# Sample attention: the new positions of a batch as columns of its first block of past positions

## The chip, the cores and the metric

The kernel runs on one core of a Trainium2 chip. Its engines work side by side, each in the order of its own instructions: PE (matrix products and turns), DVE and ACT (element work), POOL (element work and indirect loads), SP (issues loads). The metric is the device time of one launch in microseconds (us), less is better.

## The reference

One inference step of a two-layer decoder, for a prompt of 1024 positions and for a sample group of 8 batches with 8 new positions each. The change touches the second layer's attention of the sample group, which has 8 heads, so 64 query rows in a batch (8 heads by 8 positions). Keys are a latent part of 256 and a rotary part of 64, from 8192 past positions (a paged cache) and the new ones:

```python
def mla_attend(q_lat, q_rope, ckv, kr):
    nq, nk = q_lat.shape[1], ckv.shape[1]
    s = jnp.einsum('bqhc,bkc->bhqk', q_lat, ckv) + jnp.einsum('bqhr,bkr->bhqk', q_rope, kr)
    visible = jnp.arange(nk)[None, :] <= (nk - nq + jnp.arange(nq))[:, None]
    s = jnp.where(visible, s.astype(jnp.float32) * SM_SCALE, -jnp.inf)
    pr = jax.nn.softmax(s, axis=-1).astype(ckv.dtype)
    return jnp.einsum('bhqk,bkc->bqhc', pr, ckv)
...
past_ckv = cache_ckv[page_table, j].reshape(bsz, n_past, KV_LORA).astype(ckv.dtype)
o_lat = mla_attend(q_lat, q_rope, jnp.concatenate([past_ckv, ckv], axis=1),
                   jnp.concatenate([past_kr, kr], axis=1))
```

## The kernel before

`sample_attention` works through items (b, J): batch b, block J. Blocks 0 to 7 are 1024 past positions each, and block 8 holds the new positions (64 columns, those of all batches, with `mnew` masking all but the batch's own); it comes first in its batch. So 72 items. A number is kept as a high and a low part (`split`, `lo`; a low part is the number less its high part), so most products are made of several matmuls. The softmax runs over the blocks with a running maximum and sum, kept as columns of `sts`.

An item is cut into pieces, each a few instructions:
- `f` (POOL) gathers a block 2 items ahead into `raws`; `na` (ACT) and `np` (POOL) copy its high part into `khi`, `lp` (POOL, L2216, two halves of 128x1024) its low part into `klo`.
- `t0`, `t1` (PE, L2226) turn the two halves of the latent keys, `tr` (L2241) the rotary keys, into PSUM; `h0`, `h1`, `hr` (ACT) copy the high parts out, `l0`, `l1`, `lr` (DVE, `lo`, L216) the low parts. lr's row reads `L216 ... fieldC<-ps,fieldC 64x1024`. The three turns take two wide PSUM buffers in turn, so t1 needs the buffer that the tr before it filled, when hr and lr have read it.
- `s0`, `s1` (PE) are the scores of 512 columns each; `c0`, `c1` (ACT) copy the half of the low parts out, `m0`, `m1` (DVE, L2286) add and take the maximum; `nm` (DVE, L2291) turns it into the exponent's bias, `ex` (ACT, L2296) is the exponent with its sum, `al`, `ac` the factor for what came before, `su` (ACT, L2308) the running sum.
- `pt` (PE, L2321) turns the probabilities into the one "pt" buffer of PSUM, `ph` (ACT, L2326) and `pl` (DVE) read them out, `pv` (PE, L2342) multiplies with the values, `o` (DVE, L2350) adds to the batch's output.
- After block 7, `e0` (DVE, L2360 to L2362) divides by the sum, `e1`, `ec`, `e2` turn the result and store it.

The order of the pieces is one table for all engines, and in each step piece x with number d works on the item d steps back. Each engine then works strictly in that order:

```python
"m1.4 l0.2 t1.2 ph.5 pv.6 nm.4 h1.2 s0.3 l1.2 na.3 tr.2 pl.5 s1.3 ex.4 o.6 e1.8 ec.8 t0.1 e2.8 "
"f.0 np.3 hr.2 e0.6 c0.3 c1.3 su.5 ac.5 lr.2 pt.4 al.4 lp.3 h0.1 m0.3"
```

So in one step e0 of a batch's last item (6 steps back) stands on DVE ahead of lr (2 steps back), and `su` of the next item (5 steps back) stands between them. `np` overwrites what pv three blocks earlier read, and waits for it. The end of the attention overlaps with the first loads and casts of the output projection (`then`; L225 and L226 are its split).

Of the kernel before, what the change touches and what calls it, by code (L numbers as in the profile page):

```python
# [20 lines left out]
P = 128  # L21
# [1633 lines left out]
class Layer1(Layer0):  # L1655
# [501 lines left out]
    def sample_attention(self, then):  # L2157
# [15 lines left out]
        L = slice(64, 128)  # L2173
        items = [(b, J) for b in range(NB) for J in (8, 0, 1, 2, 3, 4, 5, 6, 7)]
        blk = {it: n for n, it in enumerate(it for it in items if it[1] < 8)}

# [4 lines left out]

        def piece(name, new=True):


            def add(f):
                def run(n):
                    b, J = items[n]
                    if J < 8 or new:
                        f(n, b, J, blk.get(items[n]))

                pieces[name] = run
                return f

            return add


        @piece("f", False)
        def _(n, b, J, i):
            if i > 1:
                self.gather(i)  # L2200
# [3 lines left out]

        @piece("na", False)
        def _(n, b, J, i):
            nc.scalar.copy(khi[i % 3][:, :on_a], raws[i % 4][:, :on_a])  # L2207

        @piece("np", False)
# [3 lines left out]
        @piece("lp", False)  # L2213
        def _(n, b, J, i):
            for c in (slice(0, 1024), slice(1024, 2048)):
                nc.gpsimd.tensor_tensor(klo[i % 3][:, c], raws[i % 4][:, c], khi[i % 3][:, c], op=ALU.subtract)  # L2216


        for k in range(2):

            @piece(f"t{k}", False)
# [6 lines left out]
            @piece(f"h{k}", False)  # L2228
            def _(n, b, J, i, k=k):
                nc.scalar.copy(kT[i % 2][0][:, k], live[n, "t", k])  # L2230

            @piece(f"l{k}", False)
            def _(n, b, J, i, k=k):
                self.lo(kT[i % 2][1][:, k], live[n, "t", k], kT[i % 2][0][:, k])

        @piece("tr", False)
# [7 lines left out]
        @piece("hr", False)  # L2244
        def _(n, b, J, i):
            nc.scalar.copy(rT[i % 2][:64], live[n, "t", 2][:64])  # L2246

        @piece("lr", False)
        def _(n, b, J, i):
            self.lo(rT[i % 2][64:], live[n, "t", 2][:64], rT[i % 2][:64])  # L2250


        stat = lambda n, j: sts[n % 4][:, j : j + 1]
        width = lambda J: 1024 if J < 8 else NS
        for a in range(2):
            cs = slice(a * 512, a * 512 + 512)

            @piece(f"s{a}", a == 0)
            def _(n, b, J, i, a=a, cs=cs):
                W = 512 if J < 8 else NS  # L2260
                ps = live[n, "s", a] = self.ps("s")[:, :W]
                for k in range(2):
                    for t in range(2):
                        x = kT[i % 2][t][:, k, cs] if J < 8 else ckN[:, t, k]
                        nc.tensor.matmul(ps, q(k, b), x, start=k + t == 0, stop=False)  # L2265
                qr = QRs[:, b].rearrange("p s m -> p (s m)")
                if J < 8:
                    nc.tensor.matmul(ps, qr, rT[i % 2][:, cs], start=False, stop=True)  # L2268
                else:
                    for t in range(2):  # L2270
                        nc.tensor.matmul(ps, qr[:64], krN[:64, t], start=False, stop=t == 1)

            @piece(f"c{a}", a == 0)
            def _(n, b, J, i, a=a, cs=cs):
                o = sb[n % 3][H, cs][:, : min(512, width(J))]
                nc.scalar.copy(o, live[n, "s", a][L])

            @piece(f"m{a}", a == 0)
            def _(n, b, J, i, a=a, cs=cs):

                o, ps = sb[n % 3][H, cs][:, : min(512, width(J))], live[n, "s", a]
                if J == 8:
                    tt(o, o, mnew[H, b], op=ALU.add)
                first = -3e38 if J == 8 else stat(n, 5)[H] if a else stat(n - 1, 2)[H]
                out = stat(n, 2 if a or J == 8 else 5)
                V.tensor_tensor_reduce(o, ps[H], o, op0=ALU.add, op1=ALU.max, accum_out=out[H], scale=1.0, scalar=first)  # L2286

# [5 lines left out]
        @piece("ex")  # L2293
        def _(n, b, J, i):
            o = sb[n % 3][H, : width(J)]
            nc.scalar.activation(o, o, AF.Exp, bias=stat(n, 0)[H], scale=SCALE, accum_out=stat(n, 4 if J == 8 else 3)[H])  # L2296

        @piece("al", False)
        def _(n, b, J, i):
            nc.scalar.activation(stat(n, 1)[H], stat(n - 1, 0)[H], AF.Exp, bias=stat(n, 0)[H], scale=-1.0)  # L2300

        @piece("ac", False)
        def _(n, b, J, i):
            V.tensor_copy(stat(n, 1)[L], stat(n, 1)[H])

        @piece("su", False)
        def _(n, b, J, i):
            nc.scalar.activation(stat(n, 4)[H], stat(n - 1, 4)[H], AF.Identity, bias=stat(n, 3)[H], scale=stat(n, 1)[H])  # L2308


        def spans(n, J):
            nt, K = (8, P) if J < 8 else (1, NS)
            P3 = PTb[n % 3].rearrange("p (t s q) -> p t s q", t=8, s=2)
            return nt, K, P3[:K, :nt, 0], P3[:K, :nt, 1]

        @piece("pt")
        def _(n, b, J, i):
            nt, K, *_ = spans(n, J)
            ps = self.ps("pt")
            for t in range(nt):  # L2320
                nc.tensor.transpose(ps[:K, t * 64 : t * 64 + 64], sb[n % 3][H, t * P : t * P + K], self.ident[H, H])  # L2321
            live[n, "p"] = ps[:K, : nt * 64].rearrange("p (t q) -> p t q", t=nt)

        @piece("ph")
        def _(n, b, J, i):
            nc.scalar.copy(spans(n, J)[2], live[n, "p"])  # L2326

        @piece("pl")
        def _(n, b, J, i):
            *_, hi, lo = spans(n, J)  # L2330
            self.lo(lo, live[n, "p"], hi)

        @piece("pv")
        def _(n, b, J, i):
            o = live[n, "o"] = self.ps("o")[:, :256]
            PT = PTb[n % 3]
            for t in range(8 if J < 8 else 1):
                for s in range(2):
                    x, y = PT[:, t * P : t * P + P], (khi, klo)[s][(i or 0) % 3][:, t * 256 : t * 256 + 256]
                    if J == 8:  # L2340
                        x, y = PT[:NS, :P], self.kn[:NS, s]
                    nc.tensor.matmul(o, x, y, start=t + s == 0, stop=t + s == (8 if J < 8 else 1))  # L2342

        @piece("o")
        def _(n, b, J, i):
            O = oa[b % 2]
            if J == 8:
                nc.scalar.copy(O, live[n, "o"])
            else:
                V.scalar_tensor_tensor(O, O, stat(n, 1), live[n, "o"], op0=ALU.mult, op1=ALU.add)  # L2350
# [4 lines left out]

        @piece("e0", False)
        @last
# [5 lines left out]

        @piece("e1", False)
        @last
# [164 lines left out]
```

## Time and profile before

| what | value |
|---|---|
| three runs | 3080.94, 3076.39, 3082.41 us (median 3080.94) |
| the profiled execution | 3075.58 us, span of its instructions 3073.8 us |
| granted clock of PE, mean | 0.981 |
| busy over the span | PE 97%, DVE 75%, ACT 52%, POOL 41% |
| sample attention | about 1680 to 2210 us of the span |

The profiled execution is one launch, 5.4 us below the median. A busy share over the whole span mixes stages with different limits, so the attention is read by itself. PE's busy time counts matmuls that overlap as one stretch.

### The profile page before, as it was taken

The page shows a single profiled execution, that of the slowest core. Times are in us where ns is not written, and L with a number is a line of the kernel's source. Part 1 is how long each engine was busy: PE and PEld are TensorE (multiplying, and loading weights), DVE is VectorE, ACT ScalarE, POOL GpSimd, SP SyncE. Part 2 cuts the span into 40 slices and gives each one's busy share as a digit, 9 for nine tenths or more (in the row PEclk, how much of TensorE's full clock was granted, in tenths as well). Part 3 has the DMA queues.
Part 4 walks back from the last instruction along what each step waited for, and adds up shares of the span by engine and source line. Part 5 has one row for each costly group of instructions (what it writes and reads, how often), then busy time and mean ns, then how long its engine had stood idle before and what let it go on. Part 6 is the DMA issues. An engine that isn't in the chain of part 4 may idle for free.

```text
span 3073.8 us, 51474 instructions
## 1 busy us (share of the span) xinstructions
PE 2977.0 (97%) x19503; PEld 2698.0 (88%) x19503; DVE 2299.1 (75%) x4068; ACT 1608.3 (52%) x2917; POOL 1254.5 (41%) x1207
## 2 busy tenths in 40 slices
PE   8999999899999999999999999999998999999998
PEld 7888787899999887798998888888877999998887
DVE  8753656898988776647666877777758988987766
ACT  3434644544444444345555888888735444444432
POOL 1652530466665100001112988888503666662000
PEclk9999899899999999999999999999999999999999
DMA  3223132222222676511002444444532222225775
GB/s 142 73 56 113 53 131 75 77 78 71 85 78 77 203 230 230 176 52 31 30 30 95 172 161 149 156 173 169 188 103 70 85 78 71 81 74 185 230 230 187
DMA packets 147884, 364.71 MB, mean 119 GB/s; under 512 B 28028, under 2 KB 83516, under 8 KB 139444
## 3 DMA queue, kind: packets, MB, share of 16 engines
q1 hardware_dynamic: 136336, 276.40, 27.7%
q0 software_dynamic: 9216, 83.89, 7.6%
q8 instruction: 153, 2.51, 0.3%
q10 hardware_dynamic: 2084, 1.14, 0.1%
q14 instruction: 95, 0.78, 0.1%
HBM read 302.07 MB, written 58.11 MB: 117 GB/s over the span
## 4 chain that ended last, share of the span: by engine, by line
PE 82%; DVE 7%; ACT 6%; DMA 3%; POOL 1%; issue 1%; ACTq 0%; SPq 0%; DVEq 0%; POOLq 0%
PE ps L211 20%; PE ps L212 20%; PE ps L213 20%; PE ps L2342 4%; PE ps L2265 3%; PE ps L2226 3%; DMA fieldF<-w_dn 2%; PE ps L2241 2%; DVE fieldC L216 1%; ACT fieldC L2246 1%; PE ps L514 1%; PE ps L2024 1%; PE ps L1993 1%; PE ps L2321 1%; PE ps L2268 1%
## 5 line engine op out<-in xcount | busy, mean ns | idle before, releaser
L211 PE MATMUL ps<-fieldC,fieldE 128*128 128x512 f32 (+2 forms) x916 | 338.7, 370 | 4.2 <-ACT fieldC L225 2.3
L212 PE MATMUL ps<-fieldC,fieldE 128*128 128x512 f32 (+2 forms) x916 | 338.5, 370 | 2.7 <-DVE fieldC L226 2.7
L213 PE MATMUL ps<-fieldC,fieldE 128*128 128x512 f32 (+2 forms) x916 | 338.4, 370 | 1.1 <-DVE fieldE L216 1.1
L212 PE MATMUL ps<-fieldB,fieldE 128*128 128x272 f32 (+4 forms) x872 | 276.0, 317 | 0.0
L226 DVE TENSOR_TENSOR fieldC<-fieldF,fieldC 128x1024 fp32r<-128x1024 f32 x132 | 161.3, 1223 | 124.5 <-ACT fieldC L225 123.8
L225 ACT CAST fieldC<-fieldF 128x1024 fp32r<-128x1024 f32 x132 | 138.4, 1051 | 198.5 <-DMA fieldF<-w_dn 173.0
L211 PEld LDWEIGHTS ps<-fieldC,fieldE 128*128 128x128 f32 x916 | 173.0, 189 | 33.3 <-ACT fieldC L225 3.6
L212 PEld LDWEIGHTS ps<-fieldC,fieldE 128*128 128x128 f32 x916 | 172.7, 189 | 31.4 <-DVE fieldC L226 4.1
L213 PEld LDWEIGHTS ps<-fieldC,fieldE 128*128 128x128 f32 x916 | 172.8, 189 | 30.4 <-DVE fieldE L216 2.6
L211 PE MATMUL ps<-fieldA,fieldE 128*128 128x362 f32 (+4 forms) x560 | 181.1, 325 | 7.7 <-ACT fieldA L940 7.4
L213 PE MATMUL ps<-fieldA,fieldE 128*128 128x362 f32 (+4 forms) x560 | 181.7, 324 | 0.0
L216 DVE TENSOR_TENSOR fieldC<-ps,fieldC 64x1024 fp32r<-64x1024 f32 (+4 forms) x145 | 127.8, 882 | 69.4 <-ACT fieldC L2246 63.8
L212 PEld LDWEIGHTS ps<-fieldB,fieldE 128*128 128x128 f32 x872 | 169.1, 194 | 1.8 <-DVE fieldB L941 0.5
L216 DVE TENSOR_TENSOR fieldE<-fieldF,fieldE 128x512 fp32r<-128x512 f32 (+4 forms) x265 | 137.0, 533 | 41.5 <-ACT fieldE L499 28.8
L216 DVE TENSOR_TENSOR fieldD<-ps,fieldE 128x1024 fp32r<-128x1024 f32 x128 | 154.8, 1215 | 8.7 <-ACT fieldE L2230 8.7
L420 DVE SCALAR_TENSOR_TENSOR fieldD<-fieldD,fieldF 128x480 f32<-128x480 f32 (+1 forms) x176 | 145.0, 860 | 19.4 <-ACT fieldD L418 19.4
L420 DVE SCALAR_TENSOR_TENSOR fieldA<-fieldA,fieldF 128x480 f32<-128x480 f32 (+1 forms) x176 | 144.7, 858 | 19.6 <-ACT fieldA L418 19.6
L211 PE MATMUL ps<-fieldC,fieldH 128*128 128x272 f32 x528 | 153.9, 291 | 3.3 <-ACT fieldC L346 2.9
L212 PE MATMUL ps<-fieldC,fieldH 128*128 128x272 f32 x528 | 154.0, 292 | 1.8 <-DVE fieldC L347 1.8
L2216 POOL TENSOR_TENSOR fieldB<-fieldA,fieldB 128x1024 fp32r<-128x1024 f32 x64 | 152.4, 2399 | 3.8 <-ACT fieldB L2207 1.4
L213 PE MATMUL ps<-fieldC,fieldH 128*128 128x272 f32 x528 | 153.4, 291 | 0.0
L211 PE MATMUL ps<-fieldB,fieldE 128*128 128x272 f32 (+2 forms) x488 | 146.6, 301 | 0.9 <-ACT fieldA L291 0.8
(705 smaller groups left out, 10160.4 us busy)
## 6 DMA issues: line engine op xcount, KB each, us to landing
fieldF<-w_dn SPq DMA_DIRECT2D x132, 512.0 KB, 3.8
fieldF<-w_up SPq DMA_DIRECT2D x44, 512.0 KB, 3.6
fieldF<-act SPq DMA_DIRECT2D x88, 192.0 KB, 4.1
fieldA<-w_up SPq DMA_DIRECT2D x22, 512.0 KB, 3.5
fieldD<-w_up SPq DMA_DIRECT2D x22, 512.0 KB, 3.6
fieldF<-w_in SPq DMA_DIRECT2D x16, 512.0 KB, 4.3
fieldF<-w_out SPq DMA_DIRECT2D x32, 256.0 KB, 3.2
xm<-fieldC SPq DMA_DIRECT2D x16, 512.0 KB, 2.6
```

Source lines behind the costliest of these rows:

```text
L211: mm(out, wh, xh, start=first, stop=False, **kw)
L212: mm(out, wh, xl, start=False, stop=False, **kw)
L213: mm(out, wl, xh, start=False, stop=last, **kw)
L216: self.nc.vector.tensor_tensor(out, full, hi, op=ALU.subtract)
L225: self.nc.scalar.copy(hi, raw)
L226: (eng or self.nc.vector).tensor_tensor(lo, raw, hi, op=ALU.subtract)
L420: V.scalar_tensor_tensor(y[:, :n], x[:, tap : tap + n], c(tap), y[:, :n], op0=ALU.mult, op1=ALU.add)
L2216: nc.gpsimd.tensor_tensor(klo[i % 3][:, c], raws[i % 4][:, c], khi[i % 3][:, c], op=ALU.subtract)
L2226: nc.tensor.transpose(ps[:, t * P : t * P + P], raws[i % 4][:, c : c + P], self.ident)
L2241: nc.tensor.transpose(ps[:64, t * P : t * P + P], raws[i % 4][:, c : c + 64], self.ident)
L2265: nc.tensor.matmul(ps, q(k, b), x, start=k + t == 0, stop=False)
L2342: nc.tensor.matmul(o, x, y, start=t + s == 0, stop=t + s == (8 if J < 8 else 1))
```

## The change

Block 8 is no item of its own any more: 64 items. Its work goes into the pieces of block 0:
- `s0` of block 0 first makes the 64 columns of scores of the new positions in an "s" buffer, copies and masks them into `sn`, takes their maximum as column 7, from which block 0's maximum goes on.
- `ex` of block 0 makes a second exponent over `sn` (sum in column 6); `su` of block 0 adds columns 3 and 6 on DVE (L2307), where blocks 1 to 7 still use ACT; `al` and `ac` fall away for block 0.
- `pt` of block 0 turns `sn` first, copies the two parts into `PTn`, then turns the eight tiles of the block, out of the same "pt" buffer.
- `pv` of block 0 has two matmuls more; `o` of block 0 is a copy by ACT, as it was for block 8.
- `sts` has 6 buffers in place of 4.

The diff, cut to its core:

```diff
-        items = [(b, J) for b in range(NB) for J in (8, 0, 1, 2, 3, 4, 5, 6, 7)]
-        blk = {it: n for n, it in enumerate(it for it in items if it[1] < 8)}
+        items = [(b, J) for b in range(NB) for J in range(8)]
...
+        stat = lambda n, j: sts[n % 6][:, j : j + 1]
+
+        def added(o, ps, first, out):
+
+            V.tensor_tensor_reduce(o, ps[H], o, op0=ALU.add, op1=ALU.max, accum_out=out[H], scale=1.0, scalar=first)
+
         for a in range(2):
             cs = slice(a * 512, a * 512 + 512)
 
-            @piece(f"s{a}", a == 0)
+            @piece(f"s{a}")
             def _(n, b, J, i, a=a, cs=cs):
-                W = 512 if J < 8 else NS
-                ps = live[n, "s", a] = self.ps("s")[:, :W]
+                qr = QRs[:, b].rearrange("p s m -> p (s m)")
+                if a == J == 0:
+                    ps, o = self.ps("s")[:, :NS], sn[H]
+                    for k in range(2):
+                        for t in range(2):
+                            nc.tensor.matmul(ps, q(k, b), ckN[:, t, k], start=k + t == 0, stop=False)
+                    for t in range(2):
+                        nc.tensor.matmul(ps, qr[:64], krN[:64, t], start=False, stop=t == 1)
+                    nc.scalar.copy(o, ps[L])
+                    tt(o, o, mnew[H, b], op=ALU.add)
+                    added(o, ps, -3e38, stat(n, 7))
+                ps = live[n, "s", a] = self.ps("s")
                 for k in range(2):
                     for t in range(2):
-                        x = kT[i % 2][t][:, k, cs] if J < 8 else ckN[:, t, k]
-                        nc.tensor.matmul(ps, q(k, b), x, start=k + t == 0, stop=False)
-                qr = QRs[:, b].rearrange("p s m -> p (s m)")
-                if J < 8:
-                    nc.tensor.matmul(ps, qr, rT[i % 2][:, cs], start=False, stop=True)
-                else:
-                    for t in range(2):
-                        nc.tensor.matmul(ps, qr[:64], krN[:64, t], start=False, stop=t == 1)
-
-            @piece(f"c{a}", a == 0)
+                        nc.tensor.matmul(ps, q(k, b), kT[i % 2][t][:, k, cs], start=k + t == 0, stop=False)
+                nc.tensor.matmul(ps, qr, rT[i % 2][:, cs], start=False, stop=True)
+
+            @piece(f"c{a}")
             def _(n, b, J, i, a=a, cs=cs):
-                o = sb[n % 3][H, cs][:, : min(512, width(J))]
-                nc.scalar.copy(o, live[n, "s", a][L])
-
-            @piece(f"m{a}", a == 0)
+                nc.scalar.copy(sb[n % 3][H, cs], live[n, "s", a][L])
+
+            @piece(f"m{a}")
             def _(n, b, J, i, a=a, cs=cs):
-
-                o, ps = sb[n % 3][H, cs][:, : min(512, width(J))], live[n, "s", a]
-                if J == 8:
-                    tt(o, o, mnew[H, b], op=ALU.add)
-                first = -3e38 if J == 8 else stat(n, 5)[H] if a else stat(n - 1, 2)[H]
-                out = stat(n, 2 if a or J == 8 else 5)
-                V.tensor_tensor_reduce(o, ps[H], o, op0=ALU.add, op1=ALU.max, accum_out=out[H], scale=1.0, scalar=first)
+                first = stat(n, 5) if a else stat(n - 1, 2) if J else stat(n, 7)
+                added(sb[n % 3][H, cs], live[n, "s", a], first[H], stat(n, 2 if a else 5))
...
         @piece("ex")
         def _(n, b, J, i):
-            o = sb[n % 3][H, : width(J)]
-            nc.scalar.activation(o, o, AF.Exp, bias=stat(n, 0)[H], scale=SCALE, accum_out=stat(n, 4 if J == 8 else 3)[H])
-
-        @piece("al", False)
+            for o, j in ((sb[n % 3][H], 3), (sn[H], 6))[: 1 if J else 2]:
+                nc.scalar.activation(o, o, AF.Exp, bias=stat(n, 0)[H], scale=SCALE, accum_out=stat(n, j)[H])
+
+        @piece("al")
         def _(n, b, J, i):
-            nc.scalar.activation(stat(n, 1)[H], stat(n - 1, 0)[H], AF.Exp, bias=stat(n, 0)[H], scale=-1.0)
-
-        @piece("ac", False)
+            if J:
+                nc.scalar.activation(stat(n, 1)[H], stat(n - 1, 0)[H], AF.Exp, bias=stat(n, 0)[H], scale=-1.0)
+
+        @piece("ac")
         def _(n, b, J, i):
-            V.tensor_copy(stat(n, 1)[L], stat(n, 1)[H])
-
-        @piece("su", False)
+            if J:
+                V.tensor_copy(stat(n, 1)[L], stat(n, 1)[H])
+
+        @piece("su")
         def _(n, b, J, i):
+            if J == 0:
+                tt(stat(n, 4)[H], stat(n, 3)[H], stat(n, 6)[H], op=ALU.add)
+                return
             nc.scalar.activation(stat(n, 4)[H], stat(n - 1, 4)[H], AF.Identity, bias=stat(n, 3)[H], scale=stat(n, 1)[H])
...
+        def spans(PT, nt, K=P):
+            v = PT.rearrange("p (t s q) -> p t s q", t=nt, s=2)
+            return v[:K, :, 0], v[:K, :, 1]
+
+        def turned(x, nt, K=P):
+            ps = self.ps("pt")
+            for t in range(nt):
+                nc.tensor.transpose(ps[:K, t * 64 : t * 64 + 64], x[:, t * P : t * P + K], self.ident[H, H])
+            return ps[:K, : nt * 64].rearrange("p (t q) -> p t q", t=nt)
 
         @piece("pt")
         def _(n, b, J, i):
-            nt, K, *_ = spans(n, J)
-            ps = self.ps("pt")
-            for t in range(nt):
-                nc.tensor.transpose(ps[:K, t * 64 : t * 64 + 64], sb[n % 3][H, t * P : t * P + K], self.ident[H, H])
-            live[n, "p"] = ps[:K, : nt * 64].rearrange("p (t q) -> p t q", t=nt)
+            if J == 0:
+                self.split(*spans(PTn, 1, NS), turned(sn[H], 1, NS))
+            live[n, "p"] = turned(sb[n % 3][H], 8)
...
         @piece("pv")
         def _(n, b, J, i):
             o = live[n, "o"] = self.ps("o")[:, :256]
             PT = PTb[n % 3]
-            for t in range(8 if J < 8 else 1):
+            for t in range(8):
                 for s in range(2):
-                    x, y = PT[:, t * P : t * P + P], (khi, klo)[s][(i or 0) % 3][:, t * 256 : t * 256 + 256]
-                    if J == 8:
-                        x, y = PT[:NS, :P], self.kn[:NS, s]
-                    nc.tensor.matmul(o, x, y, start=t + s == 0, stop=t + s == (8 if J < 8 else 1))
+                    y = (khi, klo)[s][i % 3][:, t * 256 : t * 256 + 256]
+                    nc.tensor.matmul(o, PT[:, t * P : t * P + P], y, start=t + s == 0, stop=J > 0 and t + s == 8)
+            for s in range(0 if J else 2):
+                nc.tensor.matmul(o, PTn[:NS], self.kn[:NS, s], start=False, stop=s == 1)
 
         @piece("o")
         def _(n, b, J, i):
             O = oa[b % 2]
-            if J == 8:
+            if J == 0:
                 nc.scalar.copy(O, live[n, "o"])
             else:
                 V.scalar_tensor_tensor(O, O, stat(n, 1), live[n, "o"], op0=ALU.mult, op1=ALU.add)
...
-        sts = [g("F^", 8) for _ in range(4)]
+        sts = [g("F^", 8) for _ in range(6)]
         sb = [g("F^", 1024) for _ in range(3)][::-1]
+        sn = g("F^", NS)
         PTb = [g("C", 1024) for _ in range(3)]
+        PTn = g("C", P)
```

The rows below show each engine's order in the new program and the old one. A name like `ps_17489` is a PSUM buffer, `fieldF_67` holds the columns of `sts` and the output sums (and `sn` in the new program), `fieldC_11912` the low and turned parts, `fieldH_9936` the scores and probabilities.

DVE, in the step in which one batch ends and the next begins. Before, from the low part of the last t0 to lr:

```order
L216 TENSOR_TENSOR fieldD_4497<-ps_17396,fieldE_4493 128x1024
L216 TENSOR_TENSOR fieldC_11912<-ps_17388,fieldC_11912 64x64
L2350 SCALAR_TENSOR_TENSOR fieldF_67<-fieldF_67,ps_17406 128x256
L2360 RECIPROCAL fieldF_67<-fieldF_67 64x1
L2361 COPY fieldF_67<-fieldF_67 64x1
L2362 TENSOR_SCALAR fieldF_67<-fieldF_67 128x256
L216 TENSOR_TENSOR fieldC_11912<-ps_17433,fieldC_11912 64x1024
```

And now:

```order
L216 TENSOR_TENSOR fieldD_4497<-ps_17452,fieldE_4493 128x1024
L216 TENSOR_TENSOR fieldC_11912<-ps_17437,fieldC_11912 128x8x64
L2354 SCALAR_TENSOR_TENSOR fieldF_67<-fieldF_67,ps_17462 128x256
L2364 RECIPROCAL fieldF_67<-fieldF_67 64x1
L2365 COPY fieldF_67<-fieldF_67 64x1
L2366 TENSOR_SCALAR fieldF_67<-fieldF_67 128x256
L2307 TENSOR_TENSOR fieldF_67<-fieldF_67 64x1
L216 TENSOR_TENSOR fieldC_11912<-ps_17489,fieldC_11912 64x1024
```

Between e0's scaling and lr stands the addition of block 0's two sums, and the low part of the probabilities ahead of `o` is a whole block's instead of the 64x64 piece.

PE, in the step that turns the probabilities of a batch's new positions, and DVE's part of it. Before, on PE:

```order
L2226 MATMUL ps_17371<-ident,fieldA_15833 128x128 x8
L2321 MATMUL ps_17388<-ident,fieldH_9936 64x64
L2226 MATMUL ps_17396<-ident,fieldA_15833 128x128 x8
```

Now, on PE, and under it DVE's rows from lr on:

```order
L2220 MATMUL ps_17416<-ident,fieldA_15833 128x128 x8
L2319 MATMUL ps_17433<-ident,fieldF_67 64x64
L2319 MATMUL ps_17437<-ident,fieldH_9936 128x64 x8
L2220 MATMUL ps_17452<-ident,fieldA_15833 128x128 x8
...
L216 TENSOR_TENSOR fieldC_11912<-ps_17397,fieldC_11912 64x1024
L216 TENSOR_TENSOR fieldC_11912<-ps_17433,fieldC_11912 64x64
```

The single turn and the eight turns follow each other on PE with the same buffer, and DVE's reading of the first stands behind lr.

ACT, at the end of the attention (the last exponents, and casts of the output projection, L225). Before:

```order
L2326 CAST fieldC_11912<-ps_21603 128x8x64
L225 CAST fieldA_21700<-fieldH_9936 128x1024
L2296 ACTIVATE fieldH_9936,fieldF_67<-fieldH_9936,fieldF_67 64x1024
L2308 ACTIVATE fieldF_67<-fieldF_67 64x1
L2300 ACTIVATE fieldF_67<-fieldF_67 64x1
```

And now:

```order
L2330 CAST fieldC_11912<-ps_21563 128x8x64
L225 CAST fieldE_4493<-fieldF_67 128x512
L2292 ACTIVATE fieldH_9936,fieldF_67<-fieldH_9936,fieldF_67 64x1024
L2309 ACTIVATE fieldF_67<-fieldF_67 64x1
L2297 ACTIVATE fieldF_67<-fieldF_67 64x1
L225 CAST fieldA_21660<-fieldH_9936 128x1024
```

The cast into fieldA, which overwrites what POOL's lp reads, has gone behind the last exponent, and a cast into fieldE stands ahead of it.

## Rows read from the trace of the kernel before

**Rows 1.** Windows: start:end, length, then busy time by engine, clock, DMA

```profile
1796.98:1862.51 65.53, 63.43 (x477) 56.22 (x476) 51.97 (x98) 56.21 (x95) 55.91 (x33) 1.00 0.45 162
```

**Rows 2.** Waits of PE: for whom, us in total, times, longest us

```profile
PE ps L2226 <- DVE fieldC L216: 13.6, 16, 1.0
```

**Rows 3.** In order of time, PE and ACT, one batch: start, us, instruction [idle before]

```profile
1875.43 1.09 PE L2226 MATMUL ps<-ident,fieldA 128*128 128x128 f32 x8 [0.83 <-DVE fieldC L216]
1882.42 0.24 PE L2321 MATMUL ps<-ident,fieldH 64*64 64x64 f32 x1
1882.81 1.09 PE L2226 MATMUL ps<-ident,fieldA 128*128 128x128 f32 x8
1883.82 0.21 ACT L2326 CAST fieldC<-ps 64x64 fp32r<-64x64 f32 x1
1905.91 1.09 PE L2226 MATMUL ps<-ident,fieldA 128*128 128x128 f32 x8 [1.00 <-DVE fieldC L216]
```

**Rows 4.** In order of time, PE, POOL and DVE, one regular step

```profile
1913.57 1.09 PE L2226 MATMUL ps<-ident,fieldA 128*128 128x128 f32 x8
1914.42 2.16 PE L2342 MATMUL ps<-fieldB,fieldC 128*128 128x256 f32 x16
1916.55 1.28 POOL L2211 TENSOR_SCALAR fieldB<-fieldA 128x1280 fp32r<-128x1280 f32 x1 [1.57 <-PE ps L2342]
1917.78 0.47 DVE L2350 SCALAR_TENSOR_TENSOR fieldF<-fieldF,ps 128x256 f32<-128x256 f32 x1
1917.91 4.72 POOL L2216 TENSOR_TENSOR fieldB<-fieldA,fieldB 128x1024 fp32r<-128x1024 f32 x2
1919.69 1.22 DVE L216 TENSOR_TENSOR fieldC<-ps,fieldC 64x1024 fp32r<-64x1024 f32 x1 [1.27 <-ACT fieldC L2246]
1921.22 0.98 PE L2226 MATMUL ps<-ident,fieldA 128*128 128x128 f32 x7
```

**Rows 5.** In order of time, the scaling of e0 and POOL's low part

```profile
1885.83 4.77 POOL L2216 TENSOR_TENSOR fieldE<-fieldA,fieldD 128x1024 fp32r<-128x1024 f32 x2
1887.57 0.80 DVE L2362 TENSOR_SCALAR fieldF<-fieldF 128x256 f32<-128x256 f32 x1
...
2211.40 0.35 DVE L2362 TENSOR_SCALAR fieldF<-fieldF 128x256 f32<-128x256 f32 x1
```

**Rows 6.** In order of time, other stages; then two group lines (least/median/most ns; busy, mean ns)

```profile
110.54 1.44 POOL L914 TENSOR_TENSOR fieldG<-fieldF,T 128x512 f32<-128x512 f32 x1 [1.52 <-DVE fieldC L918]
110.98 1.02 DVE L919 TENSOR_TENSOR fieldC<-fieldG,fieldD 128x4 f32<-128x4 f32 x1
...
646.35 0.71 DVE L420 SCALAR_TENSOR_TENSOR fieldA<-fieldA,fieldF 128x480 f32<-128x480 f32 x1
646.38 1.91 POOL L434 TENSOR_TENSOR fieldA<-fieldA 128x544 f32<-128x544 f32 x1 [1.41 <-ACT fieldA L433]
646.99 1.58 DVE L430 SCALAR_TENSOR_TENSOR fieldA<-fieldA,fieldF 128x64 f32<-128x64 f32 x2
...
L919 DVE TENSOR_TENSOR fieldC<-fieldG,fieldD x4: 151/168/1017, 111.0 to 244.6; 128x4 f32<-128x4 f32 x4
...
L2304 DVE COPY fieldF<-fieldF 64x1 f32<-64x1 f32 x64 | 9.4, 147 | 1.4
```

**Rows 7.** Waits of PE in order of time, and windows of low clock behind two

```profile
241.97 1.27 PE L1171 MATMUL ps<-fieldD,fieldG 64*128 64x136 f32 x4 [2.61 <-DVE fieldG L1158]
...
241.47:251.71 10.24, 9.74 (x36) 8.49 (x37) 7.26 (x17) 1.32 (x3) 5.41 (x6) 0.50 0.42 102
2200.72:2207.54 6.82, 5.91 (x28) 5.51 (x29) 3.35 (x6) 5.22 (x11) 0.00 (x0) 0.50 0.54 185
...
2201.63 1.11 PE L2321 MATMUL ps<-ident,fieldH 64*128 64x64 f32 x8 [3.55 <-ACT fieldH L2296]
2202.67 3.78 PE L2342 MATMUL ps<-fieldB,fieldC 128*128 128x256 f32 x16
```

**Rows 8.** In order of time, ACT at the end of the attention

```profile
2199.39 1.04 ACT L225 CAST fieldA<-fieldH 128x1024 fp32r<-128x1024 f32 x1 [2.07 <-POOL fieldB L2216]
2200.34 1.15 ACT L2296 ACTIVATE fieldH<-fieldH,fieldF 64x1024 f32<-64x1024 f32 x1
```

More of the change, by code (lines that the diff above doesn't have):

```diff
@@ L2180, in sample_attention, with piece @@
         live, pieces = {}, {}
-        def piece(name, new=True):
+        def piece(name):
             def add(f):
[L2186 to L2191, printed above, removed]
+                pieces[name] = lambda i: f(i, *items[i], i)
                 return f
             return add
-        @piece("f", False)
+        @piece("f")
         def _(n, b, J, i):
@@ L2203, in sample_attention @@
         on_a = self.on_a
-        @piece("na", False)
+        @piece("na")
         def _(n, b, J, i):
             nc.scalar.copy(khi[i % 3][:, :on_a], raws[i % 4][:, :on_a])
-        @piece("np", False)
+        @piece("np")
         def _(n, b, J, i):
             nc.gpsimd.tensor_scalar(khi[i % 3][:, on_a:], raws[i % 4][:, on_a:2048], 1.0, 0.0, op0=ALU.mult, op1=ALU.add)
-        @piece("lp", False)
+        @piece("lp")
         def _(n, b, J, i):
@@ L2219, in sample_attention @@
         for k in range(2):
-            @piece(f"t{k}", False)
+            @piece(f"t{k}")
             def _(n, b, J, i, k=k):
@@ L2226, in _ @@
                     nc.tensor.transpose(ps[:, t * P : t * P + P], raws[i % 4][:, c : c + P], self.ident)
-            @piece(f"h{k}", False)
+            @piece(f"h{k}")
             def _(n, b, J, i, k=k):
                 nc.scalar.copy(kT[i % 2][0][:, k], live[n, "t", k])
-            @piece(f"l{k}", False)
+            @piece(f"l{k}")
             def _(n, b, J, i, k=k):
                 self.lo(kT[i % 2][1][:, k], live[n, "t", k], kT[i % 2][0][:, k])
-        @piece("tr", False)
+        @piece("tr")
         def _(n, b, J, i):
@@ L2241, in _ @@
                 nc.tensor.transpose(ps[:64, t * P : t * P + P], raws[i % 4][:, c : c + 64], self.ident)
-        @piece("hr", False)
+        @piece("hr")
         def _(n, b, J, i):
             nc.scalar.copy(rT[i % 2][:64], live[n, "t", 2][:64])
-        @piece("lr", False)
+        @piece("lr")
         def _(n, b, J, i):
             self.lo(rT[i % 2][64:], live[n, "t", 2][:64], rT[i % 2][:64])
-        stat = lambda n, j: sts[n % 4][:, j : j + 1]
-        width = lambda J: 1024 if J < 8 else NS
+        stat = lambda n, j: sts[n % 6][:, j : j + 1]
@@ L2308, in _ @@
             nc.scalar.activation(stat(n, 4)[H], stat(n - 1, 4)[H], AF.Identity, bias=stat(n, 3)[H], scale=stat(n, 1)[H])
[L2311 to L2314, printed above, removed]
+        def spans(PT, nt, K=P):
[6 more added lines that the diff above has]
+            return ps[:K, : nt * 64].rearrange("p (t q) -> p t q", t=nt)
@@ L2325, in _ @@
         def _(n, b, J, i):
-            nc.scalar.copy(spans(n, J)[2], live[n, "p"])
+            nc.scalar.copy(spans(PTb[n % 3], 8)[0], live[n, "p"])
         @piece("pl")
         def _(n, b, J, i):
-            *_, hi, lo = spans(n, J)
+            hi, lo = spans(PTb[n % 3], 8)
             self.lo(lo, live[n, "p"], hi)
@@ L2354, in last @@
             return lambda n, b, J, i: f(n, b) if J == 7 else None
-        @piece("e0", False)
+        @piece("e0")
         @last
@@ L2362, in _ @@
             V.tensor_scalar(oa[b % 2], oa[b % 2], rl, None, op0=ALU.mult)
-        @piece("e1", False)
+        @piece("e1")
         @last
@@ L2370, in _ @@
             live[n, "e"] = ps[:, :256].rearrange("p (k s h t) -> p k s h t", k=2, s=2, h=8)
-        @piece("ec", False)
+        @piece("ec")
         @last
@@ L2375, in _ @@
             nc.scalar.copy(OL[:, :, :, b, :], live[n, "e"][:, :, 0])
-        @piece("e2", False)
+        @piece("e2")
         @last
@@ L2385, in sample_attention @@
         for name in early:
-            pieces[name](1)
+            pieces[name](0)
         yield
@@ L2402, in sample_attention @@
                 for name, d in order:
-                    if 0 <= step - d < N and not (step - d == 1 and name in early):
-                        pieces[name](step - d)
+                    n = step - d
+                    if 0 <= n < N and not (n == 0 and name in early):
+                        pieces[name](n)
         g.free()
```

## The prediction

> **What bounds the kernel now.** I read first the busy time of each engine over one whole batch of sample attention [rows 1]: of 65.53 us PE is busy 63.43, ACT 56.21, POOL 55.91 and DVE 51.97. The granted clock is 1.00. The stage is bound by PE, and what a batch can give back is work taken from PE, or the 2.1 us in which PE waits. Next I read what PE waits for [rows 2]. One group holds nearly all of it: the turns of the latent keys (L2226, t1) wait for lr, DVE's low part of the rotary keys (L216 into fieldC), 13.6 us in 16 waits. The list in order of time [rows 3] puts one of them, 0.83 us, in the step whose scores are those of the new positions, and the other, 1.00 us, in the step of e1 and ec. Then I read one regular step across the engines [rows 4]. From t1 to t1 it is 7.65 us (1913.57 to 1921.22). lr starts at 1919.69, takes 1.22, and t1 follows at 1921.22, so lr may come 0.31 us later before PE waits. On POOL, np waits for pv's end (1916.58) and starts at 1916.55; the two lp halves follow from 1917.91 to 1922.63. So POOL runs in step with pv, and is busy from 1.33 us to 6.05 us behind pv's end with lp.
>
> **What leaves PE's time as it is.** PE issues the same matmuls and turns before and after: the item of the new positions had no keys to turn, and its 6 score matmuls, its one turn and its 2 value matmuls are now inside the step of block 0 (the order rows of PE). So the change gains no PE work, only waits. The work that goes from other engines (8 of DVE's 0.47 us updates of the sum [rows 4], as many small ACT operations) lies beside PE, which has more to do than they.
>
> **Waits that go.** The step that was short of work goes, and with it the 0.83 us wait and two small ones: between the single turn's end at 1882.66 and t1 at 1882.81 there are 0.15 us [rows 3], and I count another like it for the value matmuls of that item. That is 1.1 us in a batch.
>
> **A wait that comes.** In `pt` of block 0 the single turn takes the one "pt" buffer, which ACT and DVE must read out before the eight turns may start. That turn is 0.24 us, ACT's copy of the 64x64 piece 0.21 [rows 3], DVE's part I put at the same, and DVE's stands behind lr (the order rows of DVE). Under 0.24 it cannot be; with all of it on the path it is 0.24+0.21+0.21 and three hand-overs, 0.85 at most, of which 0.24 is PE's own. I take 0.3, since t1 behind it would have waited for the same lr. So by waits alone a batch gives back 0.8 us (bounds 0.3 and 1.1).
>
> **The step that decides: `su` of block 0 and e0 share a step.** `su` of block 0 was an ACT operation and is now a DVE addition of two columns in SBUF, 64x1 (L2307). It stands between e0's scaling of the finished batch (L2366, 128x256) and lr. Two things in the trace bear on it. The first: e0's scaling takes 0.35 us at 2211.40, when POOL does nothing, but 0.80 at 1887.57, when lp's first half (1885.83, the pair 4.77) ran, and ends 0.16 us behind that half [rows 5]. The second: a DVE operation with two inputs in SBUF is held by POOL however small it is. An addition of 128x4 starts at 110.98, in the middle of POOL's product (110.54, 1.44 us), and ends at 112.00, 1.02 us long, where the least of its kind is 0.151 [rows 6]. The 64x1 copy L2304, with one input, has a mean of 0.147 over 64, beside a POOL that is busy six sevenths of the time [rows 1, 6]: such an operation isn't held. In which order the two get through is seen at 646 [rows 6]: DVE's L420 runs from 646.35, POOL's L434 comes at 646.38 and takes 1.91 (it waits for L420), and the L430 pair behind L420 takes 1.58 instead of twice 0.27. So when DVE lets go, the waiting POOL operation is next, and DVE's next one waits for its end.
>
> Put on the clock of the regular step, with pv's end as zero: `o` starts at 1.20 [rows 4], e0's two small operations and the hand-overs take it to 1.98, and lp's first half runs from 1.33 to 3.70. The scaling is held to 3.70+0.16 = 3.86. lp's second half, waiting, goes next, for 2.36, to 6.22, and L2307 is held until then. lr starts at about 6.27 instead of 3.11, 3.16 late, less the 0.31 of slack: **2.85 us of PE's wait**, in each of the 7 steps that hold both e0 and a block 0. In the kernel before the same scaling was held only 0.45, because lp was 1.74 us on when it came [rows 5]; on the clock of the regular step it comes 0.65 behind lp's start.
>
> The Trainium skill says the same of the pair (SBUF — State Buffer, Who interferes with whom): a DVE instruction with two SBUF inputs contends with a GpSimd instruction that reads SBUF, and whoever issues first has the port for the whole instruction. It names no least width. By it L2307 waits as above; the trace agrees down to 128x4, and no row has a single column.
>
> Bounds for this wait: 0 if a single column isn't held and the scaling comes early; 0.65 if only the scaling is held (lr at 3.11+0.95, less 0.31); 2.85 if both are. I take 2.85, since 128x4 is nearest. A batch is then 2.85-0.8 = 2.05 longer, and 7 of them 14.4 us.
>
> **The clock.** PE's wait of 2.61 us at 241.97 lies where the granted clock falls to 0.50 for 10.2 us, and that of 3.55 at 2201.63 where it is 0.50 for 6.8 [rows 7]; the trace has ten waits of 2.6 us or more, and each has such a stretch that begins within 2 us of its end. At 0.50 (1.2 GHz) one pv took 3.78 us, where at 2.4 GHz it takes 2.16 [rows 4, 7]. So a wait of 2.85 us likely brings a stretch at half clock. The shortest such stretch in the trace is 3.4 us and costs 1.7; one of 6.8 costs 3.4, less what lies in the wait. Bounds 0 and 3.4 each, and I take 1.8: 7 of them are 12.6 us.
>
> The Trainium skill (TensorE: Matmul & The Clock Gate, HAM oscillation) describes waits between bursts that let the clock fall, so that the next burst starts slow each time. The rows above agree; whether a wait of 2.85 in this stage does it, no row of before shows.
>
> **Start and end of the stage.** The first batch has nothing ahead of it, and its item filled waits of the start: 0 to 1.1 lost, I take 0.6. At the end PE waits 3.55 us for the last exponent, because ACT's cast of the next stage's weights (2199.39, 1.04 us) stands ahead of it and waits 2.07 for POOL [rows 8]. In the new order that cast stands behind it (the order rows of ACT), so the exponent starts 1.0 to 1.4 us earlier. With a little of the half clock saved I take 1.7 (bounds 0.9 and 4).
>
> **Sum.** 14.4+12.6+0.6-1.7 = +25.9 on the profiled 3075.58: 3101.5. The median of the runs shown is 5.4 above that execution, which would make 3106.8; I write 3104, between them. What can be told from no change is about 0.2%, 6 us.
>
> **Rivals.**
> - *Both held, and the clock stays up* (0.13): 14.4+0.6-1.7 = +13.3, 3089 to 3094. For it: the stage has not lost its clock at waits of 1.0 us [rows 1, 3]. Against it: ten of ten.
> - *Only the scaling is held* (0.13): L2307 slips through in front of lp's second half, or a single column isn't held. Then a batch is 0.65-0.8 = -0.15, 7 of them -1, and with the ends -2: 3073.5 to 3079, no change. For it: the one-input 64x1 operations are never held. Against it: 128x4, and the order at 646.
> - *The other side: nothing is held for long* (0.10). If DVE reaches e0 before lp starts (in under 1.33 us behind pv's end; `o` alone starts at 1.20, so all of it must come 0.7 earlier), a batch gains the 0.8: 7 x 0.8 and the end's 1.7, less 0.6, is -6.7, 3069 to 3074, faster.
> - *More is held* (0.06): the addition of `mnew` (64x64, two inputs) in `s0` comes behind np's end and waits for lp's first half too, up to 2.4 us more in a batch: above 3115.
>
> **Chances.** My forecast (both held, clock falls) has 0.58. It spans 7 x (0.9 to 3.0) of clock, 3094 to 3118. For eight in ten the range must also take the rival with the clock up and most of the no-change one: 3077 to 3120. Faster by over 0.2%: 0.10; within: 0.13; slower: 0.77.
>
> **What would show it.** In the new profile: L2307 at 2 us or more in 7 of 8; the scaling L2366 at about 2 us; t1 (L2220) waiting for lr by 2.5 to 3.2 us once a batch; a batch of about 69 us against 65.53; granted clock below 1.00 inside the stage; the turn of the probabilities waiting for DVE's 64x64 part; the last exponent ahead of the cast. I am wrong if L2307 is 0.15 us, or if the waits are there and the clock stays at 1.00.

## The result, and the profile after

The changed kernel takes 3107.36 us (median of 4 runs, 3105.9 to 3111.89), the kernel before 3078.66 (3074.04 to 3082.41): a ratio of 1.0096, interval 1.0077 to 1.0116. It is slower by about 29 us. The profiled execution took 3108.52 us.

The first view is the step in which one batch ends and the next begins, in order of time: seven of the rows of PE, POOL and DVE of the changed kernel (the others are left out). It answers to [rows 4, 5]:

```profile
1973.76 1.27 POOL L2205 TENSOR_SCALAR fieldD<-fieldA 128x1280 fp32r<-128x1280 f32 x1 [1.34 <-PE ps L2344]
1974.69 0.47 DVE L2354 SCALAR_TENSOR_TENSOR fieldF<-fieldF,ps 128x256 f32<-128x256 f32 x1
1975.11 4.74 POOL L2210 TENSOR_TENSOR fieldE<-fieldA,fieldD 128x1024 fp32r<-128x1024 f32 x2
1975.45 2.20 DVE L2366 TENSOR_SCALAR fieldF<-fieldF 128x256 f32<-128x256 f32 x1
1977.57 2.30 DVE L2307 TENSOR_TENSOR fieldF<-fieldF 64x1 f32<-64x1 f32 x1
1979.90 1.22 DVE L216 TENSOR_TENSOR fieldC<-ps,fieldC 64x1024 fp32r<-64x1024 f32 x1
1981.17 1.09 PE L2220 MATMUL ps<-ident,fieldF 128*128 128x128 f32 x8 [2.67 <-DVE fieldC L216]
```

Read it from POOL's row. The two halves of lp end at 1977.49 and 1979.85. The scaling (L2366) starts 0.34 us into the first half and ends at 1977.64, 0.16 behind its end. The 64x1 addition (L2307) starts there, at 1977.57, and ends at 1979.87, just behind the second half. Only then does lr run, and PE, which has had nothing to do for 2.67 us, starts t1 behind it.

How often it happens shows in DVE's and PE's groups. The first two lines are busy us and mean ns; the third is one line's least/median/most; the last two are PE's waits, in total, times, longest:

```profile
L2307 DVE TENSOR_TENSOR fieldF<-fieldF 64x1 f32<-64x1 f32 x8 | 16.2, 2029 | 0.0
L2366 DVE TENSOR_SCALAR fieldF<-fieldF 128x256 f32<-128x256 f32 x8 | 15.8, 1969 | 0.2
L2307 DVE TENSOR_TENSOR fieldF<-fieldF x8: 142/2298/2301, 1704.9 to 2185.0; 64x1 f32<-64x1 f32 x8
PE ps L2220 <- DVE fieldC L216: 27.6, 17, 2.7
PE ps L2319 <- DVE fieldC L216: 6.1, 8, 0.9
```

Seven of the eight additions are held; the least, 0.142, is the first batch's, which has no `e0` beside it. The waits for lr have doubled from 13.6 us [rows 2], and the turns of the probabilities (L2319) have a new wait, about 0.76 us in each batch.

The windows run from one held addition to the next (start:end, length, busy time by engine, clock, DMA); the last is the stretch of low clock, 0.50, in the third of them:

```profile
1908.56:1977.57 69.01, 64.57 (x477) 57.59 (x476) 54.74 (x97) 55.62 (x93) 55.77 (x33) 0.98 0.44 153
1977.57:2045.32 67.75, 63.33 (x477) 56.34 (x476) 54.64 (x97) 55.56 (x93) 55.78 (x33) 1.00 0.46 156
2045.32:2115.72 70.40, 65.98 (x477) 58.83 (x476) 54.73 (x96) 55.73 (x93) 55.74 (x33) 0.95 0.43 150
2048.06:2054.88 6.82, 5.96 (x26) 5.59 (x26) 5.47 (x10) 2.99 (x4) 1.50 (x2) 0.50 0.55 195
```

A batch without a low stretch is 67.75 us, 2.22 more than 65.53 [rows 1]. With one of 3.4 us it is 69.0 to 69.3, with one of 6.8 it is 70.40. Six of the seven waits have a low stretch that begins within 1.4 us of their end, five of 3.4 us and one of 6.8. PE's work is the same 477 matmuls; its busy time has grown only where the clock fell.

### The profile page after: what moved, and what is told of

The parts are those of the page before. It is cut to its first block, busy times and chain, and to the rows that moved or that the text cites. A ratio compares the mean times of both kernels' runs of the same rounds, so it can differ in the third digit from the quotient of the medians.

```text
span 3106.7 us, 51441 instructions
## 1 busy us (share of the span) xinstructions
PE 2990.2 (96%) x19503; PEld 2710.5 (87%) x19503; DVE 2315.7 (75%) x4052; ACT 1602.7 (52%) x2901; POOL 1253.1 (40%) x1207
## 4 chain that ended last, share of the span: by engine, by line
PE 83%; DVE 8%; ACT 4%; DMA 3%; POOL 1%; issue 1%; ACTq 0%; SPq 0%; DVEq 0%; POOLq 0%
PE ps L211 20%; PE ps L213 20%; PE ps L212 20%; PE ps L2344 4%; PE ps L2220 3%; PE ps L2272 3%; PE ps L2235 2%; DMA fieldF<-w_dn 1%; PE ps L514 1%; PE ps L2024 1%; PE ps L2319 1%; DVE fieldC L216 1%; PE ps L2273 1%; PE ps L1993 1%; PE ps L1171 1%
## 5 line engine op out<-in xcount | busy, mean ns | idle before, releaser
L225 ACT CAST fieldC<-fieldF 128x1024 fp32r<-128x1024 f32 x132 | 138.4, 1051 | 208.2 <-DMA fieldF<-w_dn 186.5
L216 DVE TENSOR_TENSOR fieldC<-ps,fieldC 128x512 fp32r<-128x512 f32 (+4 forms) x145 | 127.9, 882 | 77.6 <-ACT fieldC L2240 68.7
```

The source lines that it names most:

```text
L216: self.nc.vector.tensor_tensor(out, full, hi, op=ALU.subtract)
L225: self.nc.scalar.copy(hi, raw)
```

## The experiments

The runs are called e1 to e10; the pieces of the kernel that have such names stand in backticks.

**e1: su of block 0 back on ACT.**

```diff
-                tt(stat(n, 4)[H], stat(n, 3)[H], stat(n, 6)[H], op=ALU.add)
+                nc.scalar.activation(stat(n, 4)[H], stat(n, 6)[H], AF.Identity, bias=stat(n, 3)[H], scale=1.0)
```

> The changed kernel with one edit: block 0's sum of the two columns (su) goes back to ACT, as an Identity with one column as its bias, so DVE has no addition with two SBUF inputs between e0's scaling and lr. Theory (POOL's port): the scaling is still held about 2.2 us, but lr follows it at once; PE's wait for lr in that step falls from 2.67 to about 0.6 us, a batch from 69.2 (67.75 at full clock) to about 65.1 us, the clock stays at 1.00 in the stage, and the time is 2 us below that of before (bounds -6 to +3). Rival (the change costs by its own longer step, whatever DVE does in su): still 67 us and more in a batch, the time about 25 us above before.

Measured: 0.9999 (0.9987 to 1.0010). PE's waits for lr fall from 27.6 to 12.0 us, a batch is 65.50 (window below; 65.1 expected), and the batches keep a clock of 1.00. Without that one 64x1 addition the whole loss is gone; what is left of the change is worth nothing that can be told, and the rival is out. The scaling is held as in the change:

```profile
1830.03 2.20 DVE L2366 TENSOR_SCALAR fieldF<-fieldF 128x256 f32<-128x256 f32 x1
PE ps L2220 <- DVE fieldC L216: 12.0, 17, 1.1
1866.87:1932.37 65.50, 63.30 (x479) 56.32 (x476) 52.42 (x95) 55.80 (x94) 55.80 (x33) 1.00 0.46 161
```

**e2: su at the same place on DVE, with one tensor input.**

```diff
-                tt(stat(n, 4)[H], stat(n, 3)[H], stat(n, 6)[H], op=ALU.add)
+                V.tensor_scalar(stat(n, 4)[H], stat(n, 3)[H], stat(n, 6)[H], None, op0=ALU.add)
```

> The changed kernel with one edit: su of block 0 stays on DVE at the same place, 64x1, but reads one column as its tensor input and the other as the scalar of each partition. Theory (two tensor inputs in SBUF are held by POOL, one is not): 0.15 us each, not 2.30; PE's wait for lr about 0.75 us, a batch about 65.3, the time 1 us below before (bounds -5 to +4). Rival (every DVE operation behind the held scaling waits for POOL's next one, however many inputs it has; or a scalar counts as a second input): 2.3 us each, and the time about 28 us above before.

Measured: 1.0007 (0.9993 to 1.0021), a batch of 65.62 (65.3 expected). The same sum, at the same place, on the same engine:

```profile
L2307 DVE TENSOR_SCALAR fieldF<-fieldF 64x1 f32<-64x1 f32 x8 | 1.6, 198 | 0.0
```

0.20 us instead of 2.30. So for the addition it is neither the place nor the engine, but the second tensor input in SBUF; a column read as the scalar of each partition is not such an input. That is not the whole of what POOL holds: the scaling has one tensor input and a scalar of each partition too, and takes 2.20 us under lp, 0.35 without POOL [rows 5]. What parts it from the 64x1 form (it is 128x256) no run tests.

**e3: the scaling of `e0` on ACT, su as in the change.**

```diff
-            V.tensor_scalar(oa[b % 2], oa[b % 2], rl, None, op0=ALU.mult)
+            nc.scalar.activation(oa[b % 2], oa[b % 2], AF.Copy, scale=rl)
```

> The changed kernel with one edit: e0's scaling of 128x256 goes to ACT, su of block 0 stays the two-input addition on DVE. Theory (POOL gets the port in turns): the addition now comes while lp's first half runs and is held to its end, about 1.5 us instead of 2.3, and lp's second half doesn't hold it again; lr about 0.8 late, PE's wait about 0.5, a batch 65.0, clock 1.00, the time 2 us below before (bounds -6 to +3). Rival (the addition waits for both halves of lp, or for POOL's whole chain): held 3.5 us or more, PE's wait still above 2.5, the time 25 us above before.

Measured: 1.0012 (1.0000 to 1.0023), about 4 us above before and just over the bound of 3 that I had put, with a batch of 65.37 (65.0 expected). In place of the two holds there is one, to the end of the first half of lp (POOL, then DVE):

```profile
1892.47 4.70 POOL L2210 TENSOR_TENSOR fieldB<-fieldA,fieldB 128x1024 fp32r<-128x1024 f32 x2
1892.80 2.07 DVE L2307 TENSOR_TENSOR fieldF<-fieldF 64x1 f32<-64x1 f32 x1
```

2.07 where I expected 1.5, since it starts 0.33 us behind lp and not 0.9; the rival (both halves) is out. In these rows POOL and DVE go by turns, one instruction each, and the loss needs two DVE operations in a row that POOL holds: the first waits for one half, the second for the other.

**e4: both on ACT** (the edits of e1 and e3).

> Both edits: su of block 0 and e0's scaling on ACT; DVE has nothing in that step that POOL can hold. Theory: no wait of PE for lr in that step; left are the wait of the probabilities' turns for DVE (0.6 to 0.9) and the wait of e1's step (1.0); a batch is 64.5 us, 1.0 below before, and the time 6 us below before (bounds -10 to -2). Rival (the change gains nothing by waits): a batch 65.5 and the time that of before.

Measured: 0.9994 (0.9985 to 1.0004), 2 us less, against an expected 6; the batch is 65.00, 0.53 below before, where I expected 1.0. That is the change without any hold. It takes away waits of PE and brings a new one, that of L2319.

**e5: the kernel before, with the addition alone** (its result goes to an unused column).

```diff
-        @piece("su", False)
+        @piece("su")
         def _(n, b, J, i):
+            if J == 8:
+                tt(stat(n, 7)[H], stat(n, 2)[H], stat(n, 4)[H], op=ALU.add)
+                return
```

> The kernel before with one thing added: in the step of e0, at su's place on DVE between e0's scaling and lr, an addition of two 64x1 columns in SBUF into an unused column. Theory (POOL's port): e0's scaling ends 0.16 us behind lp's first half as before, the addition is then held through lp's second half, about 2.3 us; lr comes about 1.7 us late, PE waits for it 1.5 us, and a batch is 67.1 instead of 65.5; that wait is short of 2.6 us, so the clock stays at 1.00; 7 such steps, the time 11 us above before (bounds 8 to 14). Rival (64x1 is held only because of the longer step of the change): 0.15 us, a batch 65.6, the time that of before.

Measured: 1.0042 (1.0027 to 1.0058), 12.6 us by the medians. With nothing else of the change the addition is held through lp's second half, and PE waits 1.40 us for lr:

```profile
1890.93 0.80 DVE L2365 TENSOR_SCALAR fieldF<-fieldF 128x256 f32<-128x256 f32 x1
1891.65 2.32 DVE L2309 TENSOR_TENSOR fieldF<-fieldF 64x1 f32<-64x1 f32 x1
1895.28 1.09 PE L2226 MATMUL ps<-ident,fieldA 128*128 128x128 f32 x8 [1.40 <-DVE fieldC L216]
1894.00:1961.01 67.01, 63.63 (x475) 56.14 (x475) 54.24 (x98) 56.29 (x95) 55.95 (x32) 1.00 0.44 158
2029.00:2097.37 68.37, 64.99 (x475) 57.19 (x475) 54.20 (x99) 56.39 (x95) 55.87 (x33) 0.98 0.43 155
```

One expectation failed: I had written that the clock stays up. Four of the seven waits of 1.4 us are followed by a low stretch of 3.4 us, which makes the batch 1.36 us longer (68.37 against 67.01).

**e6: the single turn in the "o" buffer**, on top of e4.

```diff
-        def turned(x, nt, K=P):
-            ps = self.ps("pt")
+        def turned(x, nt, K=P, tag="pt"):
+            ps = self.ps(tag)
...
-                self.split(*spans(PTn, 1, NS), turned(sn[H], 1, NS))
+                self.split(*spans(PTn, 1, NS), turned(sn[H], 1, NS, "o"))
```

> su of block 0 and e0's scaling on ACT, and the single turn of the new positions' probabilities goes into the 'o' buffer of PSUM, so that the block's eight turns don't wait for its reading. Theory: the wait of the turns for DVE (0.77 a batch) goes and nothing takes its place; a batch is 64.3 us instead of 65.0, the time 10 us below before (bounds -13 to -5). Rival (the same wait comes back at the next pv, which now waits for the 'o' buffer, or at t1 for lr): a batch stays at 65.0.

Measured: 0.9969 (0.9957 to 0.9981). The wait of L2319 for DVE is gone and the batch is 64.02, 0.98 below e4. So that wait cost a batch 0.98 us, and not the 0.3 that I had put: 0.75 is the wait itself, and 0.23 is PE's busy time, which falls from 63.25 to 63.02 (windows under e7).

**e7: the turn of piece `e1` in "o" too, and the pieces `ec`, `e2` later in the table**, on top of run e6.

```diff
-            ps = self.ps("pt")
+            ps = self.ps("o")
...
-        "m1.4 l0.2 t1.2 ph.5 pv.6 nm.4 h1.2 s0.3 l1.2 na.3 tr.2 pl.5 s1.3 ex.4 o.6 e1.8 ec.8 t0.1 e2.8 "
-        "f.0 np.3 hr.2 e0.6 c0.3 c1.3 su.5 ac.5 lr.2 pt.4 al.4 lp.3 h0.1 m0.3"
+        "m1.4 l0.2 t1.2 ph.5 pv.6 nm.4 h1.2 s0.3 l1.2 na.3 tr.2 pl.5 s1.3 ex.4 o.6 e1.8 t0.1 "
+        "f.0 np.3 hr.2 ec.8 e0.6 c0.3 c1.3 su.5 ac.5 lr.2 e2.8 pt.4 al.4 lp.3 h0.1 m0.3"
```

> As the run with the turn in the 'o' buffer; e1's turn goes there too, and ec stands behind hr on ACT, e2 behind lr on DVE, so that they no longer delay the rotary keys. Theory: the wait of t1 in e1's step (1.0 us a batch) goes as well; a batch is 63.2 us, the time 18 us below before (bounds -22 to -12). Rival (PE's wait only moves to the probabilities' turns or to pv): a batch 64.3, the time as in the run with the turn alone.

Measured: 0.9946 (0.9932 to 0.9959), 3063.58 us, the fastest of all. Windows of one batch in e4, e6 and e7:

```profile
1872.50:1937.50 65.00, 63.25 (x478) 56.32 (x477) 50.40 (x94) 56.05 (x95) 55.78 (x33) 1.00 0.47 162
1873.39:1937.41 64.02, 63.02 (x478) 56.24 (x477) 50.31 (x94) 55.80 (x95) 55.80 (x33) 1.00 0.48 165
1868.47:1931.43 62.96, 62.96 (x478) 56.24 (x477) 50.38 (x94) 55.90 (x95) 55.80 (x33) 1.00 0.49 168
```

In the last PE is busy for the whole batch: no wait is left. The time is 16 to 17 us below before, where 18 were expected.

**e8: e7's edits of the table and of the turn of piece `e1`, in the kernel before.**

> The kernel before, with 72 items, and only e1's turn in the 'o' buffer, ec behind hr and e2 behind lr. It tells what the order edit is worth without the change. Theory: the wait of 1.0 us goes, a batch is 64.5 us, the time 8 us below before (bounds -10 to -4), so that the change with all edits keeps about 10 us of its own. Rival (the wait only moves): 65.5 and no change.

Measured: 0.9972 (0.9960 to 0.9984), a batch of 64.46:

```profile
1888.82:1953.28 64.46, 63.35 (x478) 56.21 (x477) 52.06 (x97) 56.34 (x94) 55.97 (x33) 1.00 0.47 164
```

So 1.07 us of the 2.57 that e7 gives back in a batch have nothing to do with the change, and 1.5 come with the change and the edits of e4 and e6, once nothing is held up.

**e9: PE kept busy during the wait**, with products whose result nobody reads.

```diff
             live[n, "p"] = turned(sb[n % 3][H], 8)
+            if J == 1 and b:
+                fill = self.ps("o")[:, :256]
+                for t in range(20):
+                    nc.tensor.matmul(fill, q(0, b), QL[1][:, :2].rearrange("p b s m -> p (b s m)"), start=True, stop=True)
```

> The changed kernel, in which PE makes 20 idle products (two constant operands, 256 columns, into the 'o' buffer, read by nobody) behind the turns of block 1's probabilities in batches 1 to 7, so in the time in which it waits for lr. The additions on DVE are held as in the change. Theory (PE's wait costs 2.2 us a batch, the low clock that follows it another 1.4 to 2.7): the products fit into the wait, the clock stays at 1.00 in the stage, every batch is 67.75 us, and the time is 16 us above before instead of 29 (bounds 12 to 20). Rival (the low clock has another cause, or the wait alone costs all): batches of 69 to 70 and the time 29 us above before.

Measured: 1.0072 (1.0054 to 1.0090). The 20 products take 2.65 us in PE's wait, the addition is held as in the change, and all periods of the batches are 67.76 to 67.79 at a clock of 1.00:

```profile
1913.09 2.65 PE L2330 MATMUL ps<-fieldE,fieldD 128*128 128x256 f32 x20
1908.31:1976.08 67.77, 65.89 (x498) 58.77 (x497) 54.69 (x96) 55.59 (x94) 55.86 (x32) 1.00 0.44 156
```

So the low clock comes from PE's idleness in the wait, and more work on PE made the kernel faster than the change (a median of 3103.1 us against 3108.16 in e10, and no run of one among those of the other). The time is 22 us above before by the ratio (17 to 28), more than the 16 expected, though the batches are as expected. In the profiled execution the stretch from the 10,000th matmul (ahead of the stage) to the 5,103rd from the end (behind it) is 651.9 us, 16 longer than before (635.6), and another 10 lie ahead of it, where the program has low stretches of its own of differing length. Over the twelve profiles the way to the 10,000th matmul takes 1628.0 to 1640.5 us, whatever the edit, so a few microseconds of the whole time say less than a batch does. Whether the 10 are there in e9's other runs isn't shown.

**e10: the change once more.**

> The changed kernel once more, on the same chip, for the stretches of low clock: if they hang on the wait's place and not on the program, their number and lengths in the stage differ from the first profile (six in seven batches, five of 3.4 us and one of 6.8), while PE's wait of 2.67 us, the holds of 2.20 and 2.30 and a batch without such a stretch (67.75) are the same.

Measured: 1.0096 (1.0078 to 1.0114). Batches of 69.18, 67.72, 69.03, 67.72, 70.38 and 69.28: the waits and the 67.7 are the same, and five of seven waits have a low stretch, not six.

## Why the prediction was right, point by point

**The wait that decides.** Two holds and PE's wait behind them were forecast at 1.9 to 2.4 us each and 2.85; they are 2.20, 2.30 and 2.67, and a batch at full clock is 2.22 longer, where the sum had 2.05. The scaling comes 0.34 us behind lp's start, not 0.65, and is held so much longer. The row that bore most was the 128x4 addition [rows 6]: a single column behaves as it did. That the waiting POOL instruction goes first when DVE lets go, read from the rows at 646, is what e3 shows from the other side. The rivals with a smaller hold are out by the group line of L2307, and by e1, where the loss goes with the addition. The rival in which more is held is out by the addition of `mnew` (least/median/most ns), a seventh of a hold:

```profile
L2267 DVE TENSOR_TENSOR fieldF<-fieldF x8: 218/317/318, 1689.4 to 2165.0; 64x64 f32<-64x64 f32 x8
```

The Trainium skill (SBUF — State Buffer, Who interferes with whom) has it that a DVE instruction with two SBUF inputs contends with a GpSimd (POOL) instruction that reads SBUF, and that one with at most one such input, outside the 2-port perf modes, does not. e2 agrees on one addition: 2.30 us and 0.20. For the scaling, which has one tensor input and was held all the same, no run here shows in which mode it ran.

**The clock.** The forecast was 1.8 us for each wait, 12.6 in all. e9 gives the price without any low stretch: 67.77 a batch. Against that the six periods of the change are 1.24 to 2.63 longer where the clock fell and the same where it didn't; in six periods that is 8.4 us, 1.4 each, and 9.8 for seven at that mean. The mechanism was right, the term a little large. The rival in which the clock stays up is out by the windows at 0.95 and 0.98.

**Waits that go and a wait that comes.** Their net was put at 0.8 us a batch; e4 measures 0.53. The term of the turns' wait was mis-sized: it is 0.75 us, and 0.98 with what e6 gives back besides, not 0.3. The one buffer is waited for through DVE's whole lr, and t1 gets nothing back from it: in e6, without that wait, t1 does not wait there. The waits that went are the 1.1 that I counted. A batch before has 2.10 us in which PE is not busy; in e4 it is 1.75 (65.00 less 63.25), of which 0.75 is the new wait. The rest of the 0.53 is 0.18 us of PE's busy time (63.43 before, 63.25 in e4), which the prediction took as unchanged; what shortens it isn't shown.

**Start and end.** The windows run, first in the kernel before and then in the change, from the 10,000th matmul to the end of the last value product, from the turns of the last block to that end, and from there to the 5,103rd matmul from the end:

```profile
1630.03:2209.61 579.58, 559.09 (x4149) 496.19 (x4148) 456.93 (x867) 482.22 (x829) 452.27 (x265) 0.99 0.44 155
2181.73:2209.61 27.88, 23.82 (x161) 21.18 (x160) 22.20 (x38) 21.29 (x39) 15.88 (x8) 0.88 0.32 106
2209.61:2265.62 56.01, 55.32 (x257) 45.04 (x256) 26.43 (x41) 15.43 (x26) 0.00 (x0) 1.00 0.55 188
...
1633.84:2238.74 604.90, 566.89 (x4146) 505.07 (x4145) 474.85 (x851) 477.37 (x813) 450.72 (x265) 0.98 0.43 149
2213.15:2238.74 25.59, 22.30 (x158) 19.74 (x157) 21.75 (x38) 20.63 (x39) 15.86 (x8) 0.93 0.35 117
2238.74:2297.12 58.38, 56.11 (x259) 45.52 (x259) 27.17 (x42) 16.26 (x27) 0.00 (x0) 1.00 0.54 179
```

The last exponent did come earlier: PE waits for it 2.12 us, not 3.55 [rows 7], and the low stretch at that wait is 3.4 us (2232.38 to 2235.79), not 6.8. The end of the attention is 2.3 us shorter by it, where 1.7 were put. But the start loses more than the 0.6 put there (the fifth block's turns come 71.2 us behind the 10,000th matmul, 69.8 before), and the beginning of the output projection takes 2.4 us more, a term that the sum did not have. In the other runs of the changed kernel that last stretch is 57.2 to 62.2 us; what lengthens it isn't shown.

**The sum.** 25.9 us were forecast and about 29 measured. Between the two fixed matmuls the profiled change is 27.7 us longer: 15.5 by the seven waits (7 x 2.22, forecast 14.4), about 9.8 by the clock (12.6), and 2.4 is left for start and end (-1.1). So the main term was right for its own reason, and that the sum came out so near is in part luck: the clock put too high and the ends too low nearly cancel. The upper end of the forecast's own span, 3118, does not follow from its terms, which give 3110, or 3115 with the 5.4 of the median.

## What to carry to other kernels

A DVE operation with two tensor inputs in SBUF can cost what POOL happens to be doing, not what it moves: 64x1 cost 2.3 us here, and written with a per-partition scalar 0.2. The 128x256 scaling with one tensor input was held as well, so one input alone is no safety. Look for such operations ahead of anything that PE waits for, above all two in a row while POOL runs long instructions. And price a wait of PE with the clock that may fall behind it: here each 2.67 us cost 1.4 more on average, and filling it with products that nobody reads gave that back in the batches (67.77 us).

## What was not expected of the hardware

Waits of 1.4 us of PE (e5) were followed by a stretch at half clock four times in seven, those of 2.67 had one five or six times in seven, those of about 1.0 in the same stage never. The scaling that ended 0.16 us behind lp's first half hardly made lp longer: the pair took 4.74 us, without it 4.72 [rows 4].
